# The S5 recurrence of a hybrid GLA/S5 step: phase tables and gate products moved from GpSimd to VectorE, data moves to ScalarE

## The chip, the cores and the metric

The kernel runs on one core of a Trainium2 chip. The metric is the device time of one launch in microseconds (us). Engines are named as the profile names them: PE (TensorE matmul), PEld (its weight load), DVE (VectorE), ACT (ScalarE), POOL (GpSimd), SP (SyncE, which issues most transfers).

## The reference

One inference step of a hybrid backbone over 640 tokens (128 of context, 512 of latents) of width 1024. The part around the change is the S5 branch; the loop over the layers, of which there is one, is left out.

```python
h = rms_norm(x, p["norm1_g"]) * (1 + scale1) + shift1
q, k, v, r, glr, u, ga, gb = jnp.split(h @ p["w_in"], SPLIT_IDX, axis=-1)
o_gla, gla_state = gla_mixer(q, k, v, r, glr, ...)
o_s5, s5_re, s5_im = s5_mixer(u, p["s5"], ...)
merged = sigmoid(ga) * (o_gla @ p["w_proj_gla"]) + sigmoid(gb) * (o_s5 @ p["w_proj_s5"])
x = x + gate1 * (merged @ p["w_out"])        # then an MLP with squared ReLU

def s5_direction(u, lam_re, lam_im, log_step, b_re, b_im, c_re, c_im, s0_re, s0_im):
    lam = lax.complex(lam_re, lam_im)
    lam_bar = jnp.exp(lam * jnp.exp(log_step)[:, None])
    b_bar = ((lam_bar - 1.0) / lam)[..., None] * lax.complex(b_re, b_im)
    bu = jnp.einsum('btgn,gpn->tbgp', u, b_bar)
    bu = bu.at[0].add(lam_bar * lax.complex(s0_re, s0_im))
    _, s = lax.associative_scan(_linear_recurrence, (lam_bar repeated over T, bu), axis=0)
    return jnp.einsum('tbgp,gnp->btgn', s, lax.complex(c_re, c_im)).real, s[-1]

y = y_forward + flip(y_backward) + d * u       # 512 wide, 32 groups, state of 64
y = gelu(y); y = y * sigmoid(y @ w_glu + b_glu)
```

## The kernel before

**Main work.** Every matmul of a projection is done as three: weights and activations are split into a rounded high part and a low rest (`whi`, `wlo` of the weights, `hh`, `hl` of the activations), and high by high, low by high and high by low are added. A weight comes in as `raw`, ACT rounds it to `whi` (L167), DVE subtracts to get `wlo` (L174). The projections run in the order u, k, q, v, glu (the gate of the S5 branch), glr (the low-rank decay inputs of the GLA branch), ps, and so on. The projection u begins as soon as the first of the eight 128-row pieces k=0..7 of the normalised input have been split (L581 on ACT, L223 on DVE); it needs two pieces for each unit, so k=6 and k=7 come last.

**The S5 branch as side tasks.** While PE does u, k, q, v, the other engines and small matmuls between the large ones compute the S5 branch in four rounds q=0..3 (eight groups each) and two directions d. Sequences are cut into 80 chunks of 8 tokens. In a round: `G` makes the powered input matrices (three instructions of 128x1152 elements, the first on POOL, two on DVE), `T` transposes them on PE (L851); `U` copies the chunks of u (`Ua`, ACT, L914) and transposes them (L920); `V` is the matmul of both; `B` fills the phase tables on POOL; `R` turns the chunk sums by the phase tables, scans them along the chunks with two DVE scans (L973, L975) and turns the states back; `C` makes the output matrices like `G`; `K` makes the matrices within a chunk, `P` writes them to HBM and reads them back in another order (`kd`); `Y` is the output matmul, `O` transposes its result (L1012). Before the first round, `lam` tasks compute the powers of `lam_bar`; `lam_p` is the long chain of small POOL instructions that ends in `p8r`, `p8i`, from which the tables are made. After the last round, `F` writes the final states, and `ys` applies gelu and splits for glu.

**What sets the order.** The class `Sides` is a greedy planner that runs while the program is built. Each task names its engine, a cost, and the tasks that it follows. `tick` moves a planner clock on with each large matmul and hands out tasks that fit. `force` empties the list at the end of a stage. The result is one fixed order for each engine, and each engine works strictly in its order; semaphores make it wait where an input is late. In the listings below and in the rows, `B`, `XA`, `XB`, `H` are the general buffers, `mm` and `aux` PSUM banks, `modc` the modulation columns.

Of the kernel before, what the change touches and what calls it, by code (L numbers as in the profile page):

```python
# [23 lines left out]
SEQ = [("u", 4), ("k", 4), ("q", 4), ("v", 8), ("glu", 2), ("glr", 1), ("ps", 4), ("r", 8), ("gb", 8),  # L24
# [104 lines left out]
class Weights:  # L129
# [25 lines left out]
    def ahead(self, w):  # L155

        while self.cut <= w and ("w", self.cut) in self.pos:
# [20 lines left out]
            self.sides.add(f"w{i}", [("S", 1.0, high), ("V", 1.15, low)], [("raw", p)], first=True)  # L178
# [30 lines left out]
def hybrid(tc, A, O):  # L209
    nc = tc.nc  # L210
# [18 lines left out]
    with contextlib.ExitStack() as ctx:  # L229
# [527 lines left out]
        def mod_next():  # L757
# [1424 lines left out]
```

## Time and profile before

| | |
|---|---|
| median of 3 runs | 1150.77 us (1149.26 to 1151.20) |
| profiled execution | 1148.16 us |
| its span in the trace | 1146.4 us, so 1.8 us lie outside it |
| mean granted PE clock | 0.979 of full |
| busy in the span | PE 1075.9, DVE 734.4, ACT 487.4, POOL 270.5 us |

Times of the rows count from the start of the span. PE is busy 94% of it, so a side engine matters only where PE waits for it. The rows are of one execution, and the sums of the prediction are made against its 1148.16 us; a difference is then put on the median, which is 2.6 us above it.

### The profile page before, as it was taken

The numbers are of one execution on the slowest core, as the hardware profiler recorded it, in microseconds if no ns is written. First come the engines' busy times: TensorE is split into PE (matmuls) and PEld (weight loads), VectorE is DVE, ScalarE is ACT, GpSimd is POOL, SyncE is SP. The second block draws the span as 40 slices with busy tenths as digits, with TensorE's granted clock in tenths as the row PEclk, the third lists the DMA queues.
The fourth block names the chain that finished last, engine by engine and source line by source line (L and its number), as shares of the span: only waits on it lengthen the run. The fifth ranks groups of instructions, "written<-read, shape, count | busy, mean of one in ns | idle before, by whom it ended". The sixth has DMA issues, their size and how long they took to land. (4 is left out here: it accounts for less than half of the span.)

```text
span 1146.4 us, 17133 instructions
## 1 busy us (share of the span) xinstructions
PE 1075.9 (94%) x6899; PEld 957.5 (84%) x6899; DVE 734.4 (64%) x1083; ACT 487.4 (43%) x798; POOL 270.5 (24%) x342
## 2 busy tenths in 40 slices
PE   9887798979999899999999998999999999999997
PEld 7676586667899798989999878989999988888886
DVE  6678987976576878864334467966666643345544
ACT  5222232131665576854222333356655543334334
POOL 7894655460020415110023021000000000000301
PEclk9998898989999999999999999999999999999999
DMA  9453435424421121223342510222222322223312
GB/s 379 163 175 118 154 92 171 131 86 170 137 72 48 49 60 57 69 97 124 93 146 79 214 58 1 75 74 75 74 78 89 114 89 77 89 74 92 111 37 92
DMA packets 42615, 119.77 MB, mean 104 GB/s; under 512 B 8204, under 2 KB 14876, under 8 KB 41512
## 3 DMA queue, kind: packets, MB, share of 16 engines
q1 hardware_dynamic: 39000, 107.81, 29.0%
q0 software_dynamic: 1520, 8.32, 2.0%
q10 hardware_dynamic: 2016, 2.56, 0.7%
q8 instruction: 54, 0.88, 0.3%
q14 instruction: 25, 0.20, 0.1%
HBM read 113.13 MB, written 5.54 MB: 104 GB/s over the span
## 5 line engine op out<-in xcount | busy, mean ns | idle before, releaser
L174 DVE TENSOR_TENSOR wlo<-raw,whi 128x1024 fp32r<-128x1024 f32 x95 | 131.4, 1383 | 66.8 <-ACT whi L167 65.6
L226 PE MATMUL mm<-hh,whi 128*128 128x320 f32 (+1 forms) x528 | 167.3, 319 | 1.8 <-DVE XB L223 1.2
L226 PE MATMUL mm<-H,whi 128*128 128x320 f32 (+2 forms) x760 | 168.8, 311 | 0.0
L226 PE MATMUL mm<-hh,wlo 128*128 128x320 f32 x512 | 159.7, 312 | 4.7 <-DVE wlo L174 4.7
L226 PE MATMUL mm<-hl,whi 128*128 128x320 f32 (+1 forms) x528 | 163.2, 311 | 0.0
L167 ACT ACTIVATE whi<-raw 128x1024 fp32r<-128x1024 f32 x96 | 100.8, 1050 | 94.8 <-DMA raw<-in_W 70.0
L214 POOL TENSOR_TENSOR B<-B,XB 128x256 f32<-128x256 f32 (+5 forms) x68 | 89.1, 1326 | 216.4 <-DVE B L214 107.5
L226 PE MATMUL mm<-whi,B 128*128 128x512 f32 x416 | 138.5, 389 | 0.0
L214 DVE TENSOR_TENSOR B<-B,B 128x320 f32<-128x320 f32 (+9 forms) x124 | 99.7, 839 | 58.2 <-ACT B L1815 50.8
L226 PEld LDWEIGHTS mm<-H,whi 128*128 128x128 f32 x760 | 126.6, 188 | 2.1
L226 PE MATMUL mm<-H,wlo 128*128 128x320 f32 (+2 forms) x380 | 117.4, 309 | 0.0
L226 PEld LDWEIGHTS mm<-hh,whi 128*128 128x128 f32 (+1 forms) x528 | 99.7, 189 | 10.2 <-ACT H L751 4.2
L226 PEld LDWEIGHTS mm<-hh,wlo 128*128 128x128 f32 x512 | 97.3, 190 | 5.4 <-DVE wlo L174 5.4
L226 PEld LDWEIGHTS mm<-hl,whi 128*128 128x128 f32 (+1 forms) x528 | 99.8, 189 | 0.4
L226 PE MATMUL mm<-B,whi 128*128 128x320 f32 x400 | 90.8, 314 | 9.0 <-ACT B L1958 4.2
L226 PEld LDWEIGHTS mm<-whi,B 128*128 128x128 f32 x416 | 78.1, 188 | 16.1
L226 PE MATMUL mm<-wlo,B 128*128 128x512 f32 x208 | 81.0, 390 | 1.0 <-DVE wlo L174 1.0
L226 PE MATMUL aux<-whi,B 128*128 128x512 f32 x224 | 79.2, 389 | 0.0
L226 PEld LDWEIGHTS mm<-B,whi 128*128 128x128 f32 x400 | 66.3, 188 | 14.3 <-ACT B L1958 6.3
L226 PEld LDWEIGHTS mm<-H,wlo 128*128 128x128 f32 x380 | 71.4, 188 | 0.0
L214 DVE TENSOR_TENSOR B<-B 64x320 f32<-64x320 f32 (+4 forms) x100 | 56.6, 574 | 9.3 <-POOL B L214 5.8
L226 PE MATMUL mm<-B,wlo 128*128 128x320 f32 x200 | 61.9, 309 | 0.0
(340 smaller groups left out, 2063.1 us busy)
## 6 DMA issues: line engine op xcount, KB each, us to landing
raw<-in_W SPq DMA_DIRECT2D x130, 512.0 KB, 3.9
raw<-in_WM SPq DMA_DIRECT2D x32, 512.0 KB, 4.7
H<-in_xT SPq DMA_DIRECT2D x4, 640.0 KB
B<-in_xt POOLq DMA_DIRECT2D x2, 1280.0 KB, 6.5
out_y<-yo SPq DMA_DIRECT2D x10, 256.0 KB, 2.0
H<-in_WM SPq DMA_DIRECT2D x2, 1024.0 KB, 7.5
B<-in_WM SPq DMA_DIRECT2D x2, 1024.0 KB
H<-in_WM SPq DMA_DIRECT2D x4, 512.0 KB, 10.5
```

Source lines behind the costliest of these rows:

```text
L167: self.nc.scalar.activation(box["hi"], self.raw[p], AF.Copy)
L174: self.nc.vector.tensor_tensor(lo, raw, hi.bitcast(F32), SUB)
L214: (e or V).tensor_tensor(o, a, b, op)
L226: PE.matmul(o, l, r, start=start, stop=stop, skip_group_check=True)
```

## The change

- **Products.** The 16 products of 128x1152 that POOL did for `G` and `C` (`s5_g1`, `s5_c1`) go to DVE, and `lam_q(0)` as well.
- **Tables.** `s5_tab(q, d)` on POOL (eight calls, six 128x256 products, copies and fills in each) becomes `s5_tab(q)` for both directions on DVE (four calls, six products of 128x512). The copies of it go to ACT (`s5_tab2`), the fills stay on POOL. The columns of `p8`, `pr8`, `rho` are put in the order (q, d, j) by three copies, of which two are new, in `lam_p`.
- **Recurrence.** In `s5_r3`, which runs for the real and the imaginary part, the two 64x320 sums on DVE become one 128x320 sum on DVE and two copies of 64x320 on ACT (`s5_rm`). Start and final states are copied by ACT (`s5_r0`, `s5_rf`); the last multiplication by `rho` moves from each round into `s5_f1`.
- **u.** The columns of the u weights are reordered on the host, the chunks are read back with the token order turned round, and PE transposes straight from them. The ACT copy `s5_ua` is gone.
- **glr.** Its 32 small matmul pairs come right behind v, ahead of the `force` that empties the list of side tasks, and glu comes behind. Before, glr came behind glu.
- **Planner.** Costs change (below). Five weights instead of four stand ahead of the first modulation weights. In a later stage `na` also follows `ra3` and `ra4`.

```diff
-SEQ = [("u", 4), ("k", 4), ("q", 4), ("v", 8), ("glu", 2), ("glr", 1), ("ps", 4), ("r", 8), ("gb", 8),
+SEQ = [("u", 4), ("k", 4), ("q", 4), ("v", 8), ("glr", 1), ("glu", 2), ("ps", 4), ("r", 8), ("gb", 8),
...
-            self.sides.add(f"w{i}", [("S", 1.0, high), ("V", 1.15, low)], [("raw", p)], first=True)
+            self.sides.add(f"w{i}", [("S", 1.05, high), ("V", 1.25, low)], [("raw", p)], first=True)
...
-            tt(prod, bb(Bv[1]), kv(Q2, d), MUL, G)
+            tt(prod, bb(Bv[1]), kv(Q2, d), MUL)
...
-            tt(prod, bb(Bv[3]), kv(YY, d), MUL, G)
+            tt(prod, bb(Bv[3]), kv(YY, d), MUL)
...
+        def s5_tab(q):
+            cols = slice(8 * q, 8 * q + 8)
+            shape = [128, 8, 8, 8]
...
+            vr_, vi_ = (tab[:, r, :, 16:80].rearrange("p c (a b) -> p c a b", a=8) for r in range(2))
+            tt(vr_, ar, br, MUL)
+            tt(tabw, ai, bi, MUL)
+            tt(vr_, vr_, tabw, SUB)
+            tt(vi_, ar, bi, MUL)
+            tt(tabw, ai, br, MUL)
+            tt(vi_, vi_, tabw, ADD)
...
-            tt(rta, vr[:, d][:, :, es], x, MUL)
+            x, y = phases(d) if im == 0 else phases(d)[::-1]
+            o = rtc if im else rta
+            tt(o, vr[:, d][:, :, es], x, MUL)
             tt(rtb, vi[:, d][:, :, es], y, MUL)
+            tt(o, o, rtb, ADD if im else SUB)
...
-                sd.add(f"Gp{q}{d}", [("G", 2.1, L(s5_g1, q, d))], ["lq0"] + last)
...
+                sd.add(f"Gp{q}{d}", [("V", 1.37, L(s5_g1, q, d))], ["lq0"] + last)
...
-                sd.add(f"B{q}{d}", [("G", 6.1, L(s5_tab, q, d))], ["lamP"] + ([f"R{p}{d}"] if q else ["c11"]))
...
+            sd.add(f"B{q}", [("V", 4.4, L(s5_tab, q)), ("S", 1.3, L(s5_tab2, q))], ["lamP"] + ([f"R{p}1", f"N{p}01", f"N{p}11"] if q else ["c11"]))
...
+        wglr = mm2()
+        wh, _ = WS.get(U_UNITS["glr"])
+        for k in range(8):
...
+                sd.tick(0.46)
         sd.force()
```

The first place is DVE while the projection u begins, ahead of the split `hl` of the piece k=6. `B_73` holds `p8`, `XB` holds `pr8`, both written by `lam_p` on POOL; `B_90` is the table. This is one piece of the difference, a row with + stands there only now:

```order
 L223 SCALAR_TENSOR_TENSOR H_72<-H_72,modc,B_82 128x512
+L214 TENSOR_TENSOR B_90<-B_73,XB 128x8x64
+L214 TENSOR_TENSOR B_90<-B_73,XB 128x512
+L214 TENSOR_TENSOR B_90<-B_90 128x8x64
+L214 TENSOR_TENSOR B_90<-B_73,XB 128x8x64
+L214 TENSOR_TENSOR B_90<-B_73,XB 128x512
+L214 TENSOR_TENSOR B_90<-B_90 128x8x64
+L223 SCALAR_TENSOR_TENSOR hl<-H_72,modc,hh 128x128
+L223 SCALAR_TENSOR_TENSOR hl<-H_72,modc,hh 128x512
+L174 TENSOR_TENSOR wlo<-raw,whi 128x1024
```

The six instructions of the first table, which wait for POOL, now stand ahead of the split of k=6, the next `wlo` and the split of k=7; before, five 128x32 instructions stood there, and none of them waited for POOL.

The second place is the end of the S5 branch on PE. `aux<-B,XA` and `aux<-B_81,B_106` are the output matmuls `Y` of the last round, `L1012` its transposes `O`, `mm` the projection v. Before:

```order
L226 MATMUL aux_2510<-B_82,XA 80x128
L226 MATMUL aux_2510<-B_81,B_106 80x128 x2
L226 MATMUL mm<-whi,hh 128x512
L226 MATMUL mm<-wlo,hh 128x512
L226 MATMUL mm<-whi,hl 128x512
...
L1012 MATMUL aux_2536<-par,B_82 128x80 x4
L1012 MATMUL aux_2542<-par,B_82 128x80 x4
```

Now (`mm<-hl,whi 64x320` is glr, `aux_2499` is `K` of the last round, `L1020` its `O`, `L1048` is `F`, `mm<-B_2609,whi` begins glu):

```order
L226 MATMUL mm<-hl,whi 64x320 x2
L226 MATMUL aux_2499<-B_81,B_107 32x128 x16
L226 MATMUL aux_2555<-B_82,XA 80x128
L226 MATMUL aux_2555<-B_81,B_106 80x128 x2
...
L1020 MATMUL aux_2583<-par,B_82 128x80 x4
L1020 MATMUL aux_2589<-par,B_82 128x80 x4
L1048 MATMUL aux_2605<-par,B_90 64x128
L226 MATMUL mm<-B_2609,whi 128x320
```

`K`, `Y`, `O` and `F` of the last round moved from between the matmuls of v to behind the last matmul of glr; nothing large stands between them and glu. The matmuls `V` of its first direction stand just ahead of glr, those of its second inside glr.

The third place is DVE in that end. `aux_2384`, `aux_2447` are the results of `V` for the two directions; `mrow` and `H_783`, `H_784` belong to other tasks; `B_91` is a product of `C`. Now, in a part of the rows from the first `V` on:

```order
L214 TENSOR_TENSOR B_106<-B_106,B_90 128x4x80 [waits DVE_49]
L214 TENSOR_TENSOR mrow<-mrow,aux_1729 128x512 [waits PE_49]
L1227 COPY H_783<-aux_2022 128x256
L1227 COPY H_784<-aux_2022 128x256
L174 TENSOR_TENSOR wlo<-raw,whi 128x1024 [waits DMAHW2_49,Activation_49]
L214 TENSOR_TENSOR B_81<-B_83,B_107 128x1152
L966 MEMSET B_106 128x2x4 [waits DVE_49]
L973 SCALAR_TENSOR_TENSOR B_106<-XB,B_106 128x324 [waits DVE_49,Pool_49]
L973 SCALAR_TENSOR_TENSOR B_106<-XB,B_106 128x324
L214 TENSOR_TENSOR B_81<-B_81,B_91 128x1152
```

The last two instructions of `C` of the last round stand between the steps of its first recurrence; behind these rows follow `K`, the rest of the first recurrence and the whole second one, all ahead of `Y`.

## Rows read from the trace of the kernel before

**Rows 1.** The page: busy time of each engine, share, instructions.

```profile
PE 1075.9 (94%) x6899; PEld 957.5 (84%) x6899; DVE 734.4 (64%) x1083; ACT 487.4 (43%) x798; POOL 270.5 (24%) x342
```

**Rows 2.** Windows: length, busy by engine, PE clock; sum of four to 292.4.

```profile
55.77:120.00 64.23, 49.05 (x382) 41.49 (x380) 50.24 (x74) 15.02 (x22) 43.77 (x67) 0.92 0.42 136
sum 236.63, PE 202.47 PEld 162.29 DVE 190.74 ACT 63.11 POOL 124.54; mean PE 50.62 PEld 40.57 DVE 47.69 ACT 15.78 POOL 31.14
```

**Rows 3.** PE timeline: start, duration, instruction, idle time before and its releaser.

```profile
75.28 0.77 PE L920 MATMUL aux<-par,B 80*128 80x80 f32 x8 [1.54 <-ACT B L914]
92.07 1.33 PE L851 MATMUL aux<-par,B 128*128 128x128 f32 x5 [9.82 <-DVE B L214]
182.29 0.79 PE L226 MATMUL aux<-wlo,hh 128*128 128x512 f32 x1 [5.38 <-DVE wlo L174]
279.11 0.42 PE L226 MATMUL aux<-B,XA 128*80 128x128 f32 x2 [0.29 <-DMA B<-kd]
```

**Rows 4.** Windows around low granted clock, first and last of five.

```profile
92.07:95.10 3.03, 3.03 (x16) 1.77 (x16) 3.03 (x2) 1.62 (x3) 2.28 (x1) 0.50 0.02 8
232.75:241.90 9.15, 6.50 (x28) 3.85 (x29) 8.97 (x10) 3.30 (x10) 8.24 (x6) 0.55 0.54 151
```

**Rows 5.** DVE groups from 60 to 296 us: busy, mean ns, idle before.

```profile
L174 DVE TENSOR_TENSOR wlo<-raw,whi 128x1024 fp32r<-128x1024 f32 x17 | 30.1, 1773 | 12.0 <-ACT whi L167 11.8
L214 DVE TENSOR_TENSOR B<-B,B 128x320 f32<-128x320 f32 x48 | 27.5, 617 | 0.0
L214 DVE TENSOR_TENSOR B<-B 64x320 f32<-64x320 f32 x32 | 18.9, 589 | 0.8
L214 DVE TENSOR_TENSOR B<-XB,B 128x1152 f32<-128x1152 f32 x8 | 14.5, 1810 | 12.7 <-PE aux L226 7.8 <-POOL B L214 4.9
L214 DVE TENSOR_TENSOR B<-B,B 128x256 f32<-128x256 f32 x12 | 9.8, 864 | 0.1
```

**Rows 6.** DVE timeline, single instructions and short runs of them.

```profile
53.27 1.01 DVE L223 SCALAR_TENSOR_TENSOR hl<-H,modc,hh 128x128 fp32r<-128x128 f32 x2
90.66 1.36 DVE L214 TENSOR_TENSOR B<-B 128x1152 f32<-128x1152 f32 x1 [3.75 <-POOL B L214]
255.89 1.68 DVE L214 TENSOR_TENSOR B<-aux,B 128x320 f32<-128x320 f32 x4 [3.53 <-PE aux L226]
259.84 1.56 DVE L973 TENSOR_TENSOR_SCAN B<-XB,B 128x324 f32<-128x324 f32 x2
271.84 0.89 DVE L214 TENSOR_TENSOR B<-B,B 128x320 f32<-128x320 f32 x2
276.80 1.23 DVE L174 TENSOR_TENSOR wlo<-raw,whi 128x1024 fp32r<-128x1024 f32 x1 [1.10 <-ACT whi L167]
92.19 3.27 DVE L174 TENSOR_TENSOR wlo<-raw,whi 128x1024 fp32r<-128x1024 f32 x1
```

**Rows 7.** POOL timeline of `lam_p`, the first table, one product.

```profile
45.99 2.09 POOL L214 TENSOR_TENSOR B<-B 128x32 f32<-128x32 f32 x3
55.71 0.77 POOL L214 TENSOR_TENSOR XB<-XB 128x32 f32<-128x32 f32 x3
68.34 2.65 POOL L214 TENSOR_TENSOR B<-B,XB 128x256 f32<-128x256 f32 x2
92.10 2.28 POOL L214 TENSOR_TENSOR B<-B,B 128x1152 f32<-128x1152 f32 x1 [1.47 <-DVE B L214]
```

**Rows 8.** Window of all of `lam_p`, columns as in the second group.

```profile
45.95:68.30 22.35, 20.26 (x116) 16.67 (x115) 17.28 (x56) 6.83 (x11) 20.41 (x62) 0.92 0.34 117
```

**Rows 9.** PE timeline: k=6 of u, starts of glu, glr and ps.

```profile
55.77 0.39 PE L226 MATMUL mm<-whi,hl 128*128 128x512 f32 x1
292.41 0.56 PE L226 MATMUL mm<-B,whi 128*128 128x320 f32 x2
307.43 0.46 PE L226 MATMUL mm<-hh,whi 128*64 128x320 f32 x2
312.12 0.46 PE L226 MATMUL mm<-B,whi 128*128 128x320 f32 x2
```

**Rows 10.** End of Y (PE), splits for glu (DVE), gate of glu (DVE, ACT).

```profile
283.95 0.60 PE L226 MATMUL aux<-B,B 128*80 128x128 f32 x4
288.96 2.28 DVE L214 TENSOR_TENSOR B<-B,B 128x640 fp32r<-128x640 f32 x3
299.53 0.83 DVE L214 TENSOR_TENSOR B<-B,B 128x640 fp32r<-128x640 f32 x1 [0.81 <-ACT B L1268]
297.07 0.80 ACT L1266 ACTIVATE B<-mm,par 128x640 f32<-128x640 f32 x1 [2.09 <-PE mm L226]
```

**Rows 11.** ACT group: copies of 128x320 from 60 to 296 us.

```profile
L925 ACT ACTIVATE XA<-aux 128x320 f32<-128x320 f32 x8 | 3.3, 442 | 0.9 <-PE aux L920 0.6
```

More of the change, by code (lines that the diff above doesn't have):

```diff
@@ L293, in hybrid @@
         WS.twin = (U_UNITS["glr"],)
-        order = [("w", i) for i in range(4)]
+        order = [("w", i) for i in range(5)]
         mods = [("m", i) for i in range(32)]
-        for i in range(4, N_UNITS):
+        for i in range(5, N_UNITS):
             order.append(("w", i))
-            if i < 20:
+            if i < 21:
                 order += mods[:2]
@@ L467, in hybrid @@
         w0_ = sm(128).rearrange("p (k c) -> p k c", k=4)
-        u2r, u2i, u4r, u4i, t3 = (sm(32) for _ in range(5))
+        u2r, u2i, u4r, u4i, t3, upr, upi = (sm(32) for _ in range(7))
+        qdj = lambda x: x.rearrange("p (q d j) -> p q d j", d=2, j=4)
+        dqj = lambda x: x.rearrange("p (d q j) -> p q d j", d=2, j=4)
         def lam_p():
@@ L761, in mod_next @@
             nmod[0] += 1
-            sd.now["PE"] += 0.9
+            sd.now["PE"] += 1.25
             sd.used = []
@@ L786, in hybrid @@
         gg = b2[:, 0:2048].rearrange("p (d g s) -> p d g s", d=2, g=8)
-        tabr, tabi = (b3[:, i * 640:(i + 1) * 640].rearrange("p (d q c) -> p d q c", d=2, q=4) for i in range(2))
-        rt1, rt2 = (b3[:, 1280 + i * 640:1280 + (i + 1) * 640] for i in range(2))
+        tab = b3[:, 0:1536].rearrange("p (r c x) -> p r c x", r=2, c=8)
+        rt = [b3[:, 1536 + i * 320:1856 + i * 320] for i in range(3)]
+        tabw = b3[:, 1536:2048].rearrange("p (c a b) -> p c a b", c=8, a=8)
         ee = b4[:, 0:1280].rearrange("p (d g c) -> p d g c", d=2, g=8)
@@ L916, in s5_ub, with phases @@
+        def phases(d):
+            return [tab[:, r, 0:4, 16:96] if d == 0 else tab[:, r, 4:8, 0:80][:, :, ::-1] for r in range(2)]
         def s5_ub(q):
@@ L1163, in hybrid @@
                 sd.add(f"Y{q}{a}", [("PE", 2.7, L(s5_y1, q, a)), ("S", 0.55, L(s5_y2, q, a))],
-                       [f"P{q}", f"R{q}0", f"R{q}1"] + ([f"O{p}0", f"O{p}1"] if q else []), 1)
+                       [f"P{q}"] + [f"N{q}{d}{im}" for d in range(2) for im in range(2)] + ([f"O{p}0", f"O{p}1"] if q else []), 1)
             for a in range(2):
@@ L1201, in hybrid @@
                 mod_next()
[L1202 removed]
+            sd.force(f"U{2 * cb + 1}.0")
             old = bki
@@ L1217, in hybrid @@
             sd.spend("V", 1.3, sd.now["PE"])
+        wglr = mm2()
+        wh, _ = WS.get(U_UNITS["glr"])
+        for k in range(8):
+            for n in range(2):
+                for c in range(2):
+                    mm(wglr[0:64, c, 0:320], wh[:, k * 64:(k + 1) * 64], (LO if n else HI)(k)[:, c * 320:(c + 1) * 320],
+                       start=(k + n == 0), stop=(k == 7 and n == 1))
+                sd.tick(0.46)
         sd.force()
@@ L1269, in hybrid @@
                     ("V", 0.75, lambda b=b, z=z: tt(ol[:, b], z, oh[:, b].bitcast(F32), SUB))])
-        wglr = mm2()
-        wh, _ = WS.get(U_UNITS["glr"])
-        for k in range(8):
-            for n in range(2):
-                for c in range(2):
-                    mm(wglr[0:64, c, 0:320], wh[:, k * 64:(k + 1) * 64], (LO if n else HI)(k)[:, c * 320:(c + 1) * 320],
-                       start=(k + n == 0), stop=(k == 7 and n == 1))
-                sd.tick(0.46)
-        evac(ogt[0:64], wglr[0:64, :, 0:320])
         glrT = big.tile([128, 640], F32R, tag="XA", name="glrT")
```

142 lines of the change are left out of this document (66 added, 76 removed).

## The prediction, made before the changed kernel ran

> **What bounds the kernel now.** I read the page first: PE is busy 94% of the span [rows 1], so time is only to be had where PE stands or runs at half clock. Then I cut the span into windows. From 312 us on, the projections that follow keep PE busy and the change hardly touches them. In 236.6 us from 55.77 (the last piece of the projection u) to 292.4 (the start of glu) PE works 202.5 [rows 2]; the missing 34 us are what the change can win. The timeline of PE names them: twelve waits, 33.9 us in all, from 75.28 to 279.11; the largest are 9.8 us for the first products `G` and 5.4 us for a `wlo`, and DVE ends nearly all of them [rows 3]. The windows around them show a second cost: behind a long wait the granted clock is at about half, and work runs slowly. 3.03 us of work at 0.50 after the first, 6.50 at 0.55 after the last of five such stretches [rows 4]; over the five, work times (1 - clock) gives about 7.5 us. Full-speed work from 55.77 to glu is thus 195.0 us.
>
> The groups of DVE show why it is late. The `wlo` takes 1.23 us alone and 1.77 in the mean, up to 3.27 in the moment when POOL runs a product; a 128x320 takes 0.445 and 0.617, a 128x1152 1.36 and 1.81 [rows 5 to 7]. At 1.2 ns for an element (from 1.23 us for 1024), a 128x256 should take 0.31 and takes 0.86. Over the counts that is 9.2 + 8.3 + 3.6 + 6.6, some 28 us of DVE's 190.7 [rows 2, 5].
>
> **What the change does to DVE.** It adds 16 products x 1.36 = 21.8, six 128x256 of `lam_q` x 0.31 = 1.9, and four tables of six 128x512, which no row shows; by the rate of `wlo` one takes 0.61, a table 3.7, four 14.8 [rows 6]. It takes away 32 sums of 64x320 (18.9) and puts in 16 of 128x320 (7.1) [rows 5, 6]. 190.7 - 28 + 21.8 + 1.9 + 14.8 - 11.8 = 189: as much as before, but the products no longer wait for another engine, and POOL has nothing left to run beside them but fills. I therefore count the waits of before as gone and put a price X on the new ones.
>
> The Trainium skill (SBUF — State Buffer, "Who interferes with whom") says why the stretch should vanish: DVE and GpSimd share one port pair, an exclusive lock. The trace agrees: the four products that read PSUM take 1.68 us [rows 6], 0.42 each, also while POOL works. By that rule all of the 28 us come back, by the rows alone at most those; the sum is the same.
>
> **Loss 1: the first table.** DVE works in order, and the first table now stands ahead of the split of k=6. It needs the end of `lam_p`. That chain runs on POOL from 45.95 to 68.3, 62 instructions [rows 8], and the first table starts at 68.34 [rows 7]. Two more copies come in (below 0.3 us each, by the 0.26 of a small instruction); on the other side, DVE stands still from 54 us on, and such instructions take 0.26 us when undisturbed and 0.70 when not [rows 7]. Bounds: 62.1, if all 62 took 0.26; 68.8, if none gained. I take 67.2, since most of the chain already runs near the low value. Table 3.7, first half of the split 0.5 (two take 1.01 [rows 6]): PE goes on at 71.4, where before it did at 55.77 [rows 9]. Queued behind the table are that split, the next `wlo` and the split of k=7, and PE waits for each, so nothing hides it: **+15.6 us**. The clock behind a long idle time adds 1.5, as 3.03 us at 0.50 did [rows 4]. The wait ahead of the first `U` remains: before, ACT's copy ended it (1.54 us [rows 3]); that copy is gone, but the transfer from HBM that it waited for is not. I leave the 1.5.
>
> **The gain.** From there to the end of v all waits fall. Of the 195.0, `Y` of the last round (279.11 to 284.5, 5.4 [rows 3, 10]) and about 2 of `K`, `O`, `F` (an estimate: two and a half times the 0.77 us of eight small transposes [rows 3]) are moved behind the end. The first `V` of the last round is therefore over at 71.4 + 1.5 + 1.5 + 187.6 + X = 262.0 + X. DVE has then some 160 of its 189 us in 190 us, the rest lies before and behind: 84% loaded, in strict order with PE. I take X = 3 of 0 to 10.
>
> **Loss 2: the last round stands alone.** Before, DVE took the result of `V` at 255.89 [rows 6], 36.5 us ahead of glu, and PE had matmuls of v to do meanwhile; now only those of glr are left, 307.43 to 312.12, 4.7 us [rows 9]. DVE has to run, in its order: first recurrence to the turn back 4 x 0.42 + 2 x 0.445 = 2.6; three small copies about 1.2 (by 1.2 ns for an element), a `wlo` 1.23, two instructions of `C` 2.7, scans 1.6, six 128x320 2.7, `K` 0.5, then the second recurrence 2.6 + 0.3 + 1.6 + 2.7 = 7.2 [rows 6]: 19.7. ACT's two 64-row copies, which no row shows, are bounded by zero and 0.44 each (the copy of 128 rows [rows 11]); I take 0.44: 0.9. The read-back of `kd` follows `K`, which ends some 10 us ahead of this; the rows show only that it ended the last short wait ahead of `Y` before (0.29 us [rows 3]), so I count it as hidden and, if it isn't, with up to 3 us. From the start of `Y` to the first split for glu it was 279.11 to 289.7, 10.6 [rows 3, 10]; the clock adds 1.5 (0 to 5.4, if all of `Y` is at half). Sum 32.7: glu starts at **294.7 + X** against 292.41. Of the 32.7, PE works 12 and stands about 20.
>
> **Loss 3: glr as cover.** glu ends 15.0 us after it starts (14.5 without a 0.5 us wait in it), 1.7 more for clock. Then its gate must run: from ACT's 297.07 to DVE's 300.36 are 3.3 us for one block [rows 10]. Before, glr lay beside that; now only the other blocks of ps do. Between 0 and 3.3 idle; I take 2, and 1 for clock. ps starts at 294.7 + 16.2 + 3 + X = 313.9 + X, before at 312.12 [rows 9].
>
> **Sum.** 313.9 + 3 - 312.1 = **+4.8 us** against the profiled 1148.16, that is 1153.0; on the median, 1155.5 us. The edits of `na` and of the weight order I cost at nothing: they shift side tasks by a place or two, beside PE's work; if that cover is gone, one `wlo` (1.23) is paid.
>
> **Rivals.**
> - *DVE becomes the bound in the rounds.* For it: 84% load, every table and product now in one strict order, and the `wlo` of the next weight queued behind recurrences (a step of 7 us). Against it: no wait on POOL is left. X = 13: 1165.5. The Trainium skill (Perfetto Trace Analysis, "Optimizing Scalar/DVE Operations") says that an engine that is saturated should be relieved, to ScalarE first; by that rule, this is where it goes, and the trace agrees so far that DVE is what PE waits for.
> - *Faster: `lam_p` ends early.* If POOL, undisturbed, runs all 62 instructions at 0.26 us, the chain is over at 62.1, PE is back 5.1 us earlier, and with X = 0 the sum is 4.8 - 5.1 - 3 = -3.3: 1147.5. It decides from about 63 on. Against it: DVE works as before until 54, and the long rows are of wider instructions.
> - *Nothing to measure:* X = 0 to 1 and the rest as said: 1152.5. A measurement tells about 0.2%, 2.3 us, from no change.
>
> **How the numbers follow.** Forecast (1153.1 to 1160) 0.37; DVE the bound (1160 to 1168) 0.20; no change 0.19; faster 0.24, where other gains than this one are counted in. Faster by over 0.2% is 0.24, within 0.19, slower 0.57. Ends: X (-3, +7), `lam_p` (-5, +1.6), the clock of `Y` (-1.5, +3.9), the gate (-2, +1.3); `kd` +3; the table at 0.69 us an instruction +0.5. Not all at one side: 1145 to 1166 holds 8 in 10. The forecast's own range is 1152 to 1160.
>
> **What would show it.** Right: PE idle for some 15 us ahead of a matmul with `hl` near 56 us, released by DVE, and DVE idle ahead of the first 128x512 table, released by POOL; every `wlo` near 1.23 and scans near 0.78; no wait of PE for `wlo` from 120 to 260; about 20 us of PE idle behind glr, in several waits for DVE; a short one at the start of ps. Wrong: PE waits of several us in the rounds, ended by DVE (X is large); a table that starts before 63 us, or a glu that starts before 292 (the gain is larger).

## The result and the profile after

The changed kernel takes 1160.38 us in the median (1157.84 to 1162.36), the kernel before 1150.64: a ratio of 1.0092, 95% interval [1.0077, 1.0106]. It is 9.7 us slower; the forecast was 4.8 slower. The profiled execution took 1157.84 us with a span of 1155.7, 9.3 above that of before. The sign was right, the size was not: the measured loss is twice the forecast one.

The page, busy time of each engine:

```profile
PE 1076.8 (93%) x6899; PEld 961.5 (83%) x6899; DVE 719.6 (62%) x1093; ACT 503.6 (44%) x850; POOL 165.3 (14%) x246
```

PE works as long as before [rows 1], POOL 105 us less, DVE 15 us less. Time was not added by work. In the timeline of PE the large waits of before [rows 3] are gone and others stand in their place; these are the large ones, with the first `U` (92.66), the first `V` of the last round (271.70) and the starts of glu (305.76) and ps (323.64):

```profile
72.09 0.79 PE L226 MATMUL mm<-whi,hl 128*128 128x512 f32 x1 [17.38 <-DVE hl L223]
92.66 1.08 PE L923 MATMUL aux<-par,H 80*128 80x80 f32 x8 [0.64 <-DMA H<-ud]
109.25 1.97 PE L855 MATMUL aux<-par,B 128*128 128x128 f32 x8 [4.66 <-DVE B L214]
159.97 0.69 PE L226 MATMUL aux<-B,XA 128*80 128x128 f32 x2 [4.82 <-DMA B<-kd]
271.70 1.33 PE L226 MATMUL aux<-XA,B 128*64 128x80 f32 x32
295.30 0.69 PE L226 MATMUL aux<-B,XA 128*80 128x128 f32 x2 [12.13 <-DMA B<-kd]
305.76 0.52 PE L226 MATMUL mm<-B,whi 128*128 128x320 f32 x1 [1.55 <-ACT B L1190]
323.64 0.56 PE L226 MATMUL mm<-B,whi 128*128 128x320 f32 x2
```

Three windows (length, busy time of PE, PEld, DVE, ACT, POOL, then the granted clock):

```profile
72.09:273.03 200.94, 189.52 (x1392) 155.04 (x1396) 149.94 (x247) 68.05 (x133) 0.55 (x6) 0.95 0.48 156
160.00:240.00 80.00, 79.46 (x583) 63.00 (x584) 61.67 (x94) 29.59 (x58) 0.37 (x4) 0.96 0.45 144
283.20:305.76 22.56, 8.17 (x57) 7.74 (x57) 11.41 (x37) 7.64 (x17) 0.91 (x2) 0.70 0.12 30
```

The 80 us from 160 to 240 are what the forecast hoped for, full but for half a microsecond, at a clock of 0.96. What was lost lies at the two ends and in two waits between. One for one:

| from ... to | forecast | trace after |
|---|---|---|
| PE goes on with k=6 | 71.4 | 72.09 |
| all waits from there to the first `V` of the last round (1.5 for the first `U` + X = 3) | 4.5 | 11.4 |
| that `V` is over | 265.0 | 273.0 |
| from there to glu | 32.7 | 32.7 (305.76) |
| from glu to ps | 19.2 | 17.9 (323.64) |
| from ps to the end, against before | 0 | -2.2 |

**The first table** went as foreseen. The end of `lam_p` on POOL, and DVE around it:

```profile
67.17 0.52 POOL L214 TENSOR_TENSOR B<-B,B 128x128 f32<-128x128 f32 x1
65.74 0.97 DVE L214 TENSOR_TENSOR B<-B,XB 128x512 f32<-128x512 f32 x1 [12.55 <-POOL B L214]
67.72 0.74 DVE L214 TENSOR_TENSOR B<-B,XB 128x512 f32<-128x512 f32 x1 [1.00 <-POOL B L214]
71.03 1.00 DVE L223 SCALAR_TENSOR_TENSOR hl<-H,modc,hh 128x128 fp32r<-128x128 f32 x2
```

DVE stands 12.55 us for POOL, begins the table with what is there, stands another 1.00 for the last power, which POOL ends at 67.69 (67.2 was forecast), and gives the split of k=6 at 71.03. One 128x512 takes 0.65 to 0.97 (0.61 forecast). That DVE is alone now is seen in its groups:

```profile
L174 DVE TENSOR_TENSOR wlo<-raw,whi 128x1024 fp32r<-128x1024 f32 x17 | 20.8, 1223 | 24.2 <-ACT whi L167 24.1
L214 DVE TENSOR_TENSOR B<-XB,B 128x1152 f32<-128x1152 f32 x16 | 21.3, 1347 | 6.1 <-PE aux L226 6.1
L214 DVE TENSOR_TENSOR B<-B,XB 128x512 f32<-128x512 f32 x16 | 10.7, 706 | 13.6 <-POOL B L214 13.6
```

`wlo` takes 1.22 where it took 1.77, a product 1.35 where it took 1.81 [rows 5]. The stretch is gone as forecast; the Trainium skill's rule of the shared port (SBUF — State Buffer, "Who interferes with whom") agrees with these rows. (The four PSUM products that the forecast quoted for it, at 255.89, ran while POOL was idle; in the whole trace of before, between 60 and 296 us, such products take 0.48 us each beside POOL, ten of them, and 0.48 without it.) And still `wlo` has 24 us of idle time ahead of it.

**The first T** (109.25, 4.66 us of wait). SP, ACT and DVE ahead of it:

```profile
82.58 2.30 SPq L1152 DMA_DIRECT2D ud<-H  x5
88.87 2.11 SPq L1159 DMA_DIRECT2D H<-ud  x4
91.03 1.03 SPq L150 DMA_DIRECT2D raw<-in_W  x1
98.30 1.06 ACT L167 ACTIVATE whi<-raw 128x1024 fp32r<-128x1024 f32 x1 [7.16 <-DMA raw<-in_W]
99.39 1.23 DVE L174 TENSOR_TENSOR wlo<-raw,whi 128x1024 fp32r<-128x1024 f32 x1 [8.99 <-ACT whi L167]
105.17 2.63 DVE L214 TENSOR_TENSOR B<-XB,B 128x1152 f32<-128x1152 f32 x2
```

SP issues the stores of u, then the loads that read it back, and for those it stands until the stores have landed (82.58 + 2.30 to 88.87). The raw weight behind them in its queue is asked for at 91.03. ACT waits 7.16 us for it, DVE 8.99 for ACT, and `lam_q` and the first products of `G` stand behind that `wlo` on DVE. None of this was in the forecast.

**The first Y** (159.97, 4.82 us of wait). The first store to `kd` and the load that reads it back, on SP:

```profile
145.41 2.90 SPq L887 DMA_DIRECT2D kd<-B  x4
150.87 0.67 SPq L893 DMA_DIRECT2D B<-kd  x1
```

From 145.41 to 159.97 are 14.6 us; the planner counts 7.1.

**The tail.** The last sum of the last recurrence on DVE, and the copies to `ee` on ACT:

```profile
292.76 0.49 DVE L214 TENSOR_TENSOR B<-B 128x320 f32<-128x320 f32 x1
293.34 0.96 ACT L997 ACTIVATE B<-B 64x320 f32<-64x320 f32 x2 [0.36 <-DVE B L214]
```

The copies end at 294.3, and the read-back named by the profile lets `Y` begin at 295.30: two chains of almost the same length. From the end of the first `V` (273.03) to DVE's last sum (293.25) are 20.2 us, where the forecast added up 19.7 from [rows 6].

### The profile page after: what moved, and what is told of

It reads as the page before. It is cut to its first block, busy times and chain, and to the rows that moved or that the text cites. A ratio compares the mean times of both kernels' runs of the same rounds, so it can differ in the third digit from the quotient of the medians.

```text
span 1155.7 us, 17084 instructions
## 1 busy us (share of the span) xinstructions
PE 1076.8 (93%) x6899; PEld 961.5 (83%) x6899; DVE 719.6 (62%) x1093; ACT 503.6 (44%) x850; POOL 165.3 (14%) x246
## 3 DMA queue, kind: packets, MB, share of 16 engines
q1 hardware_dynamic: 39000, 107.81, 28.6%
## 5 line engine op out<-in xcount | busy, mean ns | idle before, releaser
L174 DVE TENSOR_TENSOR wlo<-raw,whi 128x1024 fp32r<-128x1024 f32 x95 | 123.6, 1301 | 73.4 <-ACT whi L167 72.2
L226 PE MATMUL mm<-hh,whi 128*128 128x320 f32 (+1 forms) x528 | 166.0, 317 | 0.6 <-DVE XB L223 0.6
L226 PE MATMUL mm<-hl,whi 128*128 128x320 f32 (+1 forms) x528 | 162.6, 310 | 0.0
L226 PE MATMUL mm<-B,whi 128*128 128x320 f32 x400 | 92.1, 318 | 10.8 <-ACT B L1972 4.2
L214 POOL TENSOR_TENSOR B<-B,XB 128x640 f32<-128x640 f32 (+5 forms) x36 | 56.4, 1585 | 190.1 <-ACT XB L1269 80.9
L226 PEld LDWEIGHTS mm<-H,wlo 128*128 128x128 f32 x380 | 71.4, 188 | 0.0
L214 DVE TENSOR_TENSOR wlo<-raw,whi 128x512 fp32r<-128x512 f32 x54 | 37.3, 690 | 30.1 <-ACT whi L1922 29.4
```

Of the source, the lines that this page charges most:

```text
L174: self.nc.vector.tensor_tensor(lo, raw, hi.bitcast(F32), SUB)
L214: (e or V).tensor_tensor(o, a, b, op)
L226: PE.matmul(o, l, r, start=start, stop=stop, skip_group_check=True)
```

## The theories

- **A**: the loss is a sum of three: the stall at the first table (17.4 + 1.5 for the clock, and, as I thought first, the wait for the first `T` behind it), waits in the rounds, the tail.
- **B**: DVE, with all products, has too much work; taking the stall away only moves the waits.
- **C**: in the fixed order other engines are the bound from the first `T` on, so that PE loses later what it gains at the start.
- **D**: not DVE's time but the places that the planner gave the tasks decide, since it counts the products on DVE.
- **E** and **F**: the queue of SP is, or is not, the cause of the first `T`'s wait. **G** and **H**: the tail is as long by DVE and ACT alone, or the read-back paces it.

## The experiments

All ratios are to the kernel before, timed on the same chip. The waits are sums over the timeline of PE, from k=6 to the first matmul of glu.

| kernel | ratio, 95% interval | wait to 100 us | 100 to 240 | 240 to glu | glu starts |
|---|---|---|---|---|---|
| before | 1 | 11.4 | 21.9 | 0.6 | 292.4 |
| changed | 1.0092 [1.0077, 1.0106] | 18.0 | 10.0 | 16.8 | 305.8 |
| e1 table behind the splits | 1.0006 [0.9993, 1.0019] | 13.4 | 8.9 | 17.8 | 300.9 |
| e2 glr behind glu | 1.0114 [1.0087, 1.0141] | 18.6 | 9.6 | 19.2 | 303.3 |
| e3 products on POOL | 1.0013 [1.0004, 1.0023] | 18.2 | 17.3 | 5.3 | 300.8 |
| e4 before, products on DVE | 1.0094 [1.0072, 1.0117] | 7.2 | 14.1 | 19.2 | 301.1 |
| f4 table behind `lam_q` | 1.0084 [1.0067, 1.0100] | 3.8 | 12.3 | 25.2 | 305.0 |
| g2 f4 + products on POOL | 0.9911 [0.9896, 0.9927] | 6.7 | 7.7 | 13.4 | 285.6 |
| g3 f4 + longer read-back | 1.0073 [1.0057, 1.0090] | 4.5 | 5.2 | 29.1 | 304.2 |
| g4 f4 + both | 0.9865 [0.9850, 0.9879] | 6.2 | 6.2 | 13.8 | 279.8 |
| h1 f4, lower costs | 1.0154 [1.0139, 1.0170] | 5.2 | 21.0 | 18.7 | 310.5 |
| h8 g4, lower costs | 0.9914 [0.9893, 0.9935] | 6.4 | 12.0 | 3.7 | 283.1 |
| h3 changed, short `lam_p` | 0.9960 [0.9947, 0.9973] | 9.1 | 5.2 | 17.4 | 292.2 |
| h9 changed, small products | 1.0069 [1.0054, 1.0084] | 18.2 | 9.7 | 16.1 | 304.6 |
| i1 changed, u by POOL's queue | 1.0023 [1.0013, 1.0034] | 19.4 | 4.9 | 16.4 | 298.5 |
| i3 g4, u by POOL's queue | 0.9867 [0.9846, 0.9888] | 5.3 | 7.0 | 11.4 | 281.2 |
| i2 changed, last read-back out | 1.0039 [1.0024, 1.0054] | 18.4 | 8.7 | 13.4 | 301.4 |

### e1: the first table behind the splits of k=6 and k=7

```diff
-sd.add(f"B{q}", [...], ["lamP"] + ([f"R{p}1", f"N{p}01", f"N{p}11"] if q else ["c11"]))
+sd.add(f"B{q}", [...], ["lamP"] + ([f"R{p}1", f"N{p}01", f"N{p}11"] if q else ["c11", "h6", "h7"]))
```

> The changed kernel, with one edge added in the planner: the first table follows the splits of k=6 and k=7. Theory A (the changed kernel loses in three places that add up: 17.4 us where PE waits for the first table, about 11 us in the rounds where raw weights and the read-back of kd come late, about 20 us of idle time behind the last V): the wait of 17.4 us ahead of k=6 falls to below 2, a new one of 0 to 4 us comes where the copies of u stand behind the table; time 13 to 18 us below the changed kernel's 1160.4, so 1143 to 1148. Theory B (DVE with all products is the bound of the whole stage): the wait only moves, PE waits for DVE in the rounds instead, and the time stays within 4 us of 1160.

Measured: 1150.26 us, 10 below the changed kernel, the same as before, between the two ranges. The table still stood in the way, now of the copies of u: DVE's stand behind it, and ACT's (L1149) stand behind ACT's copies of the table (L910), which wait 16.01 us for DVE. PE waits for ACT (PE, then ACT):

```profile
74.93 0.63 PE L226 MATMUL mm<-hh,whi 128*128 128x320 f32 x1 [13.43 <-ACT H L1149]
73.40 0.31 ACT L910 ACTIVATE B<-B 128x128 f32<-128x128 f32 x1 [16.01 <-DVE B L214]
```

13.43 us of the 17.4 remain. Two things changed at once here, since the planner also gave the later tasks other places: the wait ahead of the first `T` is gone. The stall had more behind it than I had looked for.

### f4: the first table behind `lam_q`

```diff
-... if q else ["c11"]))
+... if q else ["c11", "h7", "lq1"]))
```

> The changed kernel, with the first table behind the split of k=7 and behind the second product table of lam_q, so that it stands behind the copies of u as well (in the run before, those copies stood behind the table and PE waited 13.4 us for them). Theory A (the stall, and what it drags behind it, is about 24 us: 17.4 of wait, 1.5 of clock, 4.7 ahead of the first T): no wait above 3 us before 90 us, Y waits for kd as before, the last wait of 12 us for kd stays; 1135 to 1142. Theory B (DVE's order is full, so that what is won at the start is lost in the last round): 1147 to 1152, with a longer idle time ahead of glu.

Measured: 1158.43 us, above the ranges of both theories. The stall is gone (3.8 us of waits up to 100 us), and nothing is won. PE of this kernel in its last 20 us ahead of glu:

```profile
288.59 0.72 PE L226 MATMUL aux<-B,B 128*80 128x128 f32 x2 [4.39 <-ACT B L997]
294.15 0.72 PE L226 MATMUL aux<-B,B 128*80 128x128 f32 x2 [4.85 <-ACT B L997]
```

These are two matmuls of `Y`; ahead of them, from 249 to 270 us, PE waits four times for DVE, 1.3 to 3.1 us, at `T` and `K`. In PE's order both `T` of the last round now stand behind the last large matmul of v, where in the changed kernel about 6 and 1 us of v still came behind them: the planner, which now counts the table later, hands out the last round later, and it piles up where no main work is left. This is against A, and as B says; but a run in which the order changes as well proves neither theory.

### h3: the stall alone taken away, in the same order

```diff
-csq(u2r, u2i, upr, upi, t3, G)
... (all powers of lam_p)
+for x in (pr8[:, 2:8], pi8[:, 2:8], p8r, p8i, um):
+    G.memset(x, 0.5)
```

> The changed kernel with every engine but POOL in exactly the same order; on POOL the powers in lam_p are left out (five fills with a constant stand for them, so the states, tables and S5 results are not those of the reference), so that the first table finds its input some 15 us earlier. This takes the stall away and changes no place of any instruction. Theory A (the stall costs what the trace shows, 17.4 + 1.5, and drags 4.7 behind it): 1136 to 1141. Theory C (in the fixed order the other engines are the bound from the first T on, and PE waits elsewhere for what it gained): 1147 to 1156, with longer waits in the rounds or in the end.

Measured: 1143.87 us, 0.9960 of before and 15 below the changed kernel. PE:

```profile
58.19 0.79 PE L226 MATMUL mm<-whi,hl 128*128 128x512 f32 x1 [3.57 <-DVE hl L223]
95.58 1.97 PE L838 MATMUL aux<-par,B 128*128 128x128 f32 x8 [4.67 <-DVE B L214]
146.32 0.69 PE L226 MATMUL aux<-B,XA 128*80 128x128 f32 x2 [4.66 <-DMA B<-kd]
281.54 0.69 PE L226 MATMUL aux<-B,XA 128*80 128x128 f32 x2 [12.38 <-DMA B<-kd]
```

The kernel leaves the powers out and fills their places with a constant; the order on the other engines stays. The wait ahead of k=6 shrinks from 17.38 to 3.57, by 13.8 us; the span is 13.3 shorter, the median some 15. Everything behind keeps its waits: 4.67 for the first `T`, 4.66 for the first `Y`, 12.38 for the last. The time lies between the ranges of A and C. So in an unchanged order the stall is paid in full: C is refuted, and so is the part of A by which the stall drags the wait for the first `T` behind it (without those 4.7, A's range would have held).

### e3, e4, g2: where the products are made

```diff
-tt(prod, bb(Bv[1]), kv(Q2, d), MUL)
+tt(prod, bb(Bv[1]), kv(Q2, d), MUL, G)
...
-sd.add(f"Gp{q}{d}", [("V", 1.37, L(s5_g1, q, d))], ["lq0"] + last)
+sd.add(f"Gp{q}{d}", [("G", 2.1, L(s5_g1, q, d))], ["lq0"] + last)
```

e3 does this (and the same for `C`, whose three products become three tasks) in the changed kernel, g2 in f4 with the cost 2.3; e4 does the reverse in the kernel before.

> The changed kernel, with the 16 products of G and C back on POOL and the planner told so. The stall ahead of k=6 stays in all theories. Theory A: the last V stands some 10 us of matmuls earlier, so 5 to 10 us of the tail are covered again, but wlo and scans stretch again beside POOL (some 15 us of DVE) and PE waits for POOL or DVE in the rounds: 1153 to 1161. Theory B: without the products DVE has 22 us less and the rounds run free: 1145 to 1150.

> The kernel before, with one part of the change alone: the 16 products of G and C on DVE (planner cost 1.37), tables and all else as before. Theory A: the part itself is no loss, since DVE gets back the time that it lost beside POOL and no longer waits for it: the wait of 9.8 us ahead of the first T shrinks by 3 to 6, the waits for wlo shrink; 1141 to 1149. Theory B: 22 us more on the engine that is the bound: 1153 to 1162.

> The one before, with the products of G and C on POOL again (planner cost 2.3). The last V stands 10 us of matmuls earlier in PE's order. Theory A: as without it, less 3 to 9 us, since more of the last round is covered and the planner finds DVE less full: 1130 to 1138. Theory B': the products beside DVE stretch wlo and scans by as much as they free, no difference: within 2 us of the kernel before it in this list.

Measured: 1151.15, 1160.45 and 1138.86 us. This one part of the change costs about 9 us in the changed kernel, 11 in the kernel before and 20 in f4. e3 falls between the ranges of A and B, e4 into that of B, and g2 0.9 us above that of A; B' is wrong by 18 us. e4 has the whole loss of the change without its tables. The last wait of PE in e4:

```profile
289.88 0.69 PE L226 MATMUL aux<-B,XA 128*80 128x128 f32 x2 [12.50 <-DMA B<-kd]
```

With the products on DVE the last waits are 19.2 us (16.8 in the changed kernel); before they were 0.6. With the products on POOL in the changed kernel (e3) they are 5.3, while the waits from 100 to 240 us rise from 10.0 to 17.3, as A had said.

### h9: the same order, short products

```diff
+cut = lambda x: x[:, :, 0:1, 0:1]
-tt(prod, bb(Bv[3]), kv(YY, d), MUL)
+tt(cut(prod), cut(bb(Bv[3])), cut(kv(YY, d)), MUL)
```

The same is done in `s5_g1`, but for its first product.

> The changed kernel with the same order on all engines, but 15 of the 16 moved products work on 8 of 1152 columns each (the matrices of G and C are therefore not those of the reference). DVE has 15 x 1.3 = 19.5 us less to do, at unchanged places. Theory B (DVE's own time is the bound of the rounds): 1140 to 1146. Theory D (not DVE's time but the places that the planner gave the tasks are the bound, since it counts the products): only the waits that DVE ends become shorter, 4.7 ahead of the first T and 2.7 in the tail: 1151 to 1157.

Measured: 1157.19 us, 2.7 below the changed kernel by the ratios, whose intervals overlap (the spans differ by 0.5), although DVE is busy 16.6 us less between 72 and 305 us (154.8 against 171.4). PE:

```profile
109.06 1.97 PE L857 MATMUL aux<-par,B 128*128 128x128 f32 x8 [4.58 <-DVE B L214]
159.55 0.69 PE L226 MATMUL aux<-B,XA 128*80 128x128 f32 x2 [4.56 <-DMA B<-kd]
293.14 0.69 PE L226 MATMUL aux<-B,XA 128*80 128x128 f32 x2 [11.87 <-DMA B<-kd]
```

All large waits stay, also the one ahead of the first `T`, which D had expected to shrink. So B is refuted for the fixed order: the time of the products on DVE is not what PE waits for. What is left for the 9 to 20 us of the products are the places that the planner gives to `T`, `V`, `K` and `Y` when it counts them on DVE, as D says.

For the tail the places can be counted. Behind the second `V` of the last round, PE's order still has 87 large matmuls of v (128x512, 0.23 us each at full clock) in the kernel before, 63 in h8, 42 in e3, 30 in g4, 27 in g2, 6 in e4, 3 in h1, and none in the changed kernel, f4 and g3. The waits from 240 us to glu go with these numbers: 0.6, 3.7, 5.3, 13.8, 13.4, 19.2, 18.7, then 16.8, 25.2 and 29.1. Elsewhere D is argued by elimination: no run has the order of e3 with the products on DVE.

### h1 and h8: lower costs in the planner

```diff
-[("S", 1.05, high), ("V", 1.25, low)]
+[("S", 1.0, high), ("V", 1.15, low)]
...
-sd.add(f"Gp{q}{d}", [("V", 1.37, L(s5_g1, q, d))], ["lq0"] + last)
+sd.add(f"Gp{q}{d}", [("V", 1.3, L(s5_g1, q, d))], ["lq0", "lq1"] + last)
...
-("V", 1.37, L(s5_c1, q, d)), ("V", 1.37, L(s5_c2, q, d)), ("V", 1.4, L(s5_c3, q, d))
+("V", 1.3, L(s5_c1, q, d)), ("V", 1.3, L(s5_c2, q, d)), ("V", 1.3, L(s5_c3, q, d))
...
-("V", 3.0, L(s5_r1, q, d)), ("V", 1.8 if d == 0 else 2.2, L(s5_r2, q, d))
+("V", 2.7, L(s5_r1, q, d)), ("V", 1.5 if d == 0 else 2.0, L(s5_r2, q, d))
```

h1 changes f4 in this way, h8 the fastest version g4 (there the products stay on POOL at 2.3). Two things come with the lower costs: the first product now also follows `lq1`, and the cost of `wlo` holds for all weights of the kernel, not only for those beside the S5 branch.

> Table behind lam_q as in the earlier run of 1158.4, and the planner's DVE costs lowered by 5 to 15 per cent, to the durations of the trace (product 1.30, table 3.9, wlo 1.15, recurrence 2.7 + 1.5 or 2.0 + 2 x 1.38). No work changes; the last V stands 9 us of matmuls earlier. Theory D: 6 to 12 us below 1158.4, so 1146 to 1152. Theory B: DVE cannot follow, and PE waits as long in the rounds: 1156 to 1160.

> The fastest version so far (1133.7: table behind lam_q, products on POOL, longer read-back in the planner), with the same lowered DVE costs. The last V stands some 8 us of matmuls earlier. Theory D: 1125 to 1131. Theory B, or stretch beside POOL that the lowered costs leave out: 1132 to 1137.

Measured: 1166.78 and 1140.67 us, 8 and 6 us slower than without (by the ratios), outside the ranges of both theories and against D as I had put it. The last `V` does stand earlier; but the `Y` of h1 now wait 4 to 7 us for the read-back, the last one 12, and one large matmul of v, into an `aux` bank, 7 us for DVE (the last line is of a later stage):

```profile
141.23 0.71 PE L226 MATMUL aux<-B,XA 128*80 128x128 f32 x2 [6.25 <-DMA B<-kd]
226.78 0.76 PE L226 MATMUL aux<-whi,hh 128*128 128x512 f32 x1 [7.18 <-DVE B L214]
299.94 0.68 PE L226 MATMUL aux<-B,XA 128*80 128x128 f32 x2 [12.27 <-DMA B<-kd]
406.33 0.48 PE L226 MATMUL aux<-B 128*64 128x64 f32 x4 [2.88 <-DVE B L223]
```

In the tail the waits fall as D says, from 25.2 to 18.7 us (h1) and from 13.8 to 3.7 (h8); from 100 to 240 us they rise, from 12.3 to 21.0 and from 6.2 to 12.0. Earlier places help only as far as what they need is there. That the higher costs had held slack that covered the read-back is argued, not shown. And the loss is not one of the S5 rounds alone: in the traces glu starts 5.5 us later in h1 than in f4 and 3.4 later in h8 than in g4, and from there to the end h1 takes 6.2 and h8 4.6 us more. The last line above is one of the waits there.

### g3 and g4: a longer read-back in the planner

```diff
-("D", 3.0, L(s5_store, q)), ("D", 0.6, L(s5_toep, q)), ("D", 3.5, lambda: None)
+("D", 3.0, L(s5_store, q)), ("D", 0.6, L(s5_toep, q)), ("D", 7.0, lambda: None)
```

> The first of this list, with the planner's cost of the read-back of kd raised by 3.5 us (from 7.1 to 10.6 in all; in the changed kernel the trace has 14.6 us from the first store to the first matmul that uses it). Theory A: the waits of 4 to 5 us ahead of Y in the first rounds shrink below 2; 4 to 8 us below the first of this list. Rival: PE then runs out of main work earlier and waits as long in the last round: no difference.

> All three together: table behind lam_q, products on POOL, the cost of the read-back raised. Theory A: 1126 to 1136, the fastest of this list. If the gains hide each other, it is no better than the better of the two single steps.

Measured: 1157.97 us, no difference to f4 that the intervals show: the two waits for `kd` in the rounds fall from 9.8 to 5.0 us in sum, and the waits behind 240 us rise by 3.9, as the rival said. With the products on POOL, where the end is less crowded, the same edit wins 5 us: 1133.69, the fastest so far. DVE's `wlo` in it, and the last wait of PE:

```profile
L174 DVE TENSOR_TENSOR wlo<-raw,whi 128x1024 fp32r<-128x1024 f32 x16 | 25.2, 1576 | 17.9 <-ACT whi L167 17.9
269.37 0.72 PE L226 MATMUL aux<-B,XA 128*80 128x128 f32 x2 [8.31 <-DMA B<-kd]
```

`wlo` is stretched again to 1.58, and the kernel is 26 us faster than the one in which it takes 1.22.

### e2: glr behind glu again

```diff
-SEQ = [..., ("v", 8), ("glr", 1), ("glu", 2), ...
+SEQ = [..., ("v", 8), ("glu", 2), ("glr", 1), ...
... (the matmuls of glr and the copy of their result move behind glu)
```

> The changed kernel, with glr put back behind glu. Theory A: the tail behind V is paced by DVE and the read-back, so glr was hidden there for nothing; put back it costs its 4.7 us on PE and wins at most the 2.5 us that PE waits and runs slowly at the start of ps: 1161 to 1165. Theory B says nothing of glr: 1160. If the move of glr was itself a cause of loss (it ends the cover of the gate), the time falls by 2 us or more, to 1158 or less.

Measured: 1162.51 us, 1.0114 [1.0087, 1.0141]; the interval overlaps that of the changed kernel, so the 2 us that A has are neither shown nor refuted. That the move was itself a loss is not borne out.

### i1 and i3: the loads of u on another queue

```diff
-nc.sync.dma_start(Hs[q][0:80, 1280:2304].rearrange("p (j n) -> p j n", j=8), src)
+nc.gpsimd.dma_start(Hs[q][0:80, 1280:2304].rearrange("p (j n) -> p j n", j=8), src)
```

> The changed kernel with the same order on PE, DVE and ACT, but the four loads that read the chunks of u back are issued by POOL, not by SP. In the changed kernel SP stood from 84.9 to 91.0 us for them, and the raw weights behind them came late; DVE then stood 9.0 us ahead of a wlo, with lam_q and the first products queued behind it, and PE 4.7 us ahead of the first T. Theory E (that queue is the cause of the first T's wait): SP is free 2 to 4 us earlier, the wait falls to 0 to 2.5 us; 2 to 5 us below the changed kernel. Rival F (the raw buffer that the load needs comes free no earlier, or the transfer itself is the length of the wait): the wait stays above 3.5 us, the time within 2 us.

> The fastest version so far (1133.7) with the loads of the chunks of u on POOL's queue; its first T waits 5.6 us. Theory E: 2 to 5 us faster, 1129 to 1132. Rival F: 1133 to 1135.

Measured: 1151.60 us for i1, 0.9932 of the changed kernel (1.0023 / 1.0092), some 8 us less. SP, DVE and PE, with the first `U` and the first `T`:

```profile
86.29 0.33 SPq L150 DMA_DIRECT2D raw<-in_W  x1
91.69 1.23 DVE L174 TENSOR_TENSOR wlo<-raw,whi 128x1024 fp32r<-128x1024 f32 x1 [1.72 <-ACT whi L167]
93.60 1.30 PE L923 MATMUL aux<-par,H 80*128 80x80 f32 x8 [2.00 <-DMA H<-ud]
106.16 1.04 PE L855 MATMUL aux<-par,B 128*128 128x128 f32 x8
```

The raw weight is asked for at 86.29, not 91.03, its `wlo` runs at 91.69, not 99.39, and the first `T` has no wait at all. E holds, and wins more than its 2 to 5: with the wait of 4.66 goes the slow clock behind it (0.77 in the mean from 104.5 to 119.5 in the changed kernel). The first `U` waits 2.00 us instead of 0.64. The spans differ by 5.5 us; the profiled execution of the changed kernel is the fastest of its four, 2.5 us below their median, so the trace can't show all of the 8. In g4 the same edit (i3) gives 1132.98, ratio 0.9867 [0.9846, 0.9888], no difference: there the first `T` loses its wait of 5.58 us too, but the first `U` now waits 5.33 us for its loads, where it waited 0.62.

### i2: the last read-back left out

```diff
+if q < 3:
     nc.sync.dma_start(tm.rearrange("p i g m -> p (i g m)"), src)
```

> The changed kernel without the last of the four read-backs of kd (the output matmul of the last round uses the matrices of the round before, so a quarter of the S5 output is not that of the reference); all else as it is. The profile names that read-back for the last wait of 12.1 us. Theory G (it ends together with the recurrence on DVE and the copies on ACT, which PE needs too): the wait is then named for ACT and is shorter by 1 to 2 us; time 0 to 2 us below the changed kernel. Rival H (the read-back is what paces the tail): 6 to 10 us below.

Measured: 1153.79 us, 6 below the changed kernel. PE, from the second `V` of the last round:

```profile
274.05 1.33 PE L226 MATMUL aux<-XA,B 128*64 128x80 f32 x32 [1.56 <-DVE H L1228]
283.16 0.72 PE L226 MATMUL aux<-B,B 128*80 128x128 f32 x2 [2.75 <-ACT B L998]
290.71 0.71 PE L226 MATMUL aux<-B,B 128*80 128x128 f32 x2 [6.84 <-ACT B L998]
```

PE now waits for the copies on ACT, 2.75 and 6.84 us. From the second `V` to glu it is 27.3 us (274.05 to 301.35) against 28.6 (277.19 to 305.76): by the trace G holds for the tail. The time alone would fit H. But 3 of the 5 us between the spans lie ahead of that `V`, where the two kernels are the same: the first `Y` waits 3.63 us instead of 4.82, the half clock behind it ends at 162.6 instead of 166.0, and a wait of 0.75 at 258.79 is absent. These look like differences between two executions; why the medians too are 6 us apart is open.

## Why the prediction was wrong

- **Right: the stall at the first table.** Forecast 15.6 + 1.5 for the clock; PE goes on 16.3 us later than before, and in h3, 13.8 of its 17.4 us of wait taken away gave 13 (span) to 15 us (median). The end of `lam_p` was met to 0.5 us, by choosing near the upper bound.
- **Right in sum, in part by luck: the tail.** 32.7 us forecast, 32.7 measured. Its parts: DVE 20.2 (19.7 forecast), ACT's copies 1.1 (0.9), the read-back 1.0 (0; without it the tail is 1.3 shorter, i2), `Y` to glu 10.5 (12.1). PE stands 16 us of it, not about 20, and most of that in one wait that the profile names for the read-back, not in several for DVE.
- **Right: the waits of before vanish**, and so does the stretch beside POOL. Of the 33.9 us, 5.3 are left in their places (ahead of the first `U` and the first `T`).
- **Wrong: the new waits.** The step that failed is "I take X = 3 of 0 to 10". X is the sum of the waits from 92.66 to the first `V` of the last round, 11.4, less what stands for the first `U`: 10.8. It was sized by DVE's load (84% forecast, 149.9 of 200.9 us or 75% measured), and DVE's load has little to do with it: h9 took 16.6 us of DVE's work away in the same order, and the waits stayed. Its two large parts are a weight that SP asks for late, behind transfers for which it stands (4.66, shown by i1), and a read-back that takes 14.6 us where 7.1 are planned (4.82; in g3, made from f4, which plans it longer, such waits halve). The forecast put the new waits down to DVE; the two large ones come over SP's queue and the transfers.
- **How the sum came out all the same:** 4.8 forecast, + 0.7 for the start of k=6, + 6.9 for the waits, + 0.4 for PE's work, 0 for the tail, - 1.3 from glu to ps (of the 2 + 1 us for the gate little is seen: PE stands 0.34 us there), - 2.2 behind ps: 9.3, the difference of the spans.
- **Wrong, and hidden in the 0.4: the clock.** The forecast charged the slow clock to the stall alone, 1.5 us. Behind the two new waits of nearly 5 us PE works at half clock too; from k=6 to that `V` it is 16.68 us of work at 0.50 (windows 72.09:77.20, 109.25:114.80 and 159.97:166.00), so 8.3 us. Before, the same reading to the end of each slow stretch gives 24.56 us of work at 0.50 (92.07:97.10, 121.00:127.80, 138.10:141.50, 182.29:185.90, 233.60:243.90), so 12.3 us and not the 7.5 of the forecast, whose windows (92.07:95.10, 232.75:241.90) ended too early; its full-speed work, 195.0, should have been 190.2. The two errors, 6.8 us too little and 4.8 too much, nearly cancel, by luck.
- **The rival "DVE becomes the bound in the rounds"** gave 1165.5 for X = 13. The time lies just inside the range that I gave it (1160 to 1168), and its mechanism did not hold: in the view of waits DVE itself stands 23.6 us ahead of `wlo`, for ACT, between 99 and 260 us. The Trainium skill (Perfetto Trace Analysis, "Optimizing Scalar/DVE Operations") says that with DVE saturated, moving some work to Scalar "(or even GPSIMD)" may make sense, and that between GpSimd and DVE it might not help. Here the move of the products back to POOL does help, by 9 and 20 us (e3 and g2); but h9 shows that it isn't DVE's time that is won.
- **Also wrong in kind:** I put the products down as no loss, "as much as before". e4 shows a loss of 11 us for them alone. It appears in my sum all the same, as the tail, which I had read from the order without asking which part of the change made it.
- **Small:** from ps on, the changed kernel is 2.2 us faster than before, where I had counted nothing; most of it is one wait in the GLA stage, 2.88 us ahead of a matmul at 389.13 before, 0.69 at 400.40 after. The cost of `wlo` in the planner is the likely cause: 1.15 before, 1.25 in the change, and in h1 and h8, which put it back to 1.15, the wait is 2.88 again.

The sums of the windows at half clock, after and before, and the view of DVE's waits after (total, times, longest):

```profile
sum 16.69, PE 16.68 PEld 15.30 DVE 9.51 ACT 1.79 POOL 0.00; mean PE 5.56 PEld 5.10 DVE 3.17 ACT 0.60 POOL 0.00
sum 29.14, PE 24.56 PEld 17.93 DVE 27.72 ACT 8.71 POOL 21.26; mean PE 4.91 PEld 3.59 DVE 5.54 ACT 1.74 POOL 4.25
DVE wlo L174 <- ACT whi L167: 23.6, 10, 9.0
```

What stays open: a part of the medians' gains in i1 and i2 that the traces don't show, and which of the lowered costs loses the time in h1 and h8.

## What to carry to other kernels

In a fixed order, an engine's load says little about the waits that it makes: ask for each instruction on which the bound engine waits what stands ahead of it on its engine and on its queue, down to the transfers. Time freed on an engine is won only where something waits for it: 13.8 us less of waiting for POOL gave 13 to 15 (h3), 16.6 us less of DVE's work some 2.7, not clear of the noise (h9). A planner's costs set the places, and a cost nearer to the measured one is no gain by itself: the read-back at 10.6 instead of 7.1 won nothing in one order and 5 us in another, and lower costs for DVE lost 6 and 8. Three edits to the changed kernel (the first table behind `lam_q`, the products on POOL, and the read-back planned at 10.6) make it 1.35% faster than before; without them it is 0.9% slower.

## What was not expected of the hardware

A copy of 64x320 on ACT takes 0.48 us (two in 0.96), as much as one of 128x320 from PSUM took (0.44): half the partitions save nothing here. A read-back through HBM of a quarter of `kd` takes 14.6 us in the first round of the changed kernel and 10.8 in the tail (284.53 to 295.30), counted from the first store to the matmul that waits for it; from 153 to 160 us the DMA engines are busy 0.52 of the time, in the tail 0.12. And half the speed behind a wait lasts: from 159 to 166 us, after the wait of 4.82, PE was busy 6.03 us at a granted clock of 0.51, so that a wait of 5 us cost 8. Behind the wait of 4.56 in h9 the half clock ended at 162.4 already: the price of a wait of this size is not the same in every execution.
